# Two halves of the tensor engine for products of 64 rows or columns, and single-pass compressed scores, in a two-block transformer kernel

## The chip, the cores and the metric

The kernel runs on one core of a Trainium2 chip. The metric is the device time of one execution in microseconds (us). The core has a matrix engine (TensorE, PE in the profile, with PEld for the loads of its stationary operand), VectorE (DVE), ScalarE (ACT) and DMA queues that SyncE (SP) issues; GpSimd (POOL) is idle here. Products land in PSUM, in eight banks of 128 partitions by 512 float32 columns.

## The reference, cut to what matters

256 tokens of width 1024 pass through two blocks. The first block mixes tokens with gated linear attention, a convolution and differential attention, then applies routed experts. The second block has two layers, each an FFN, a token mixer and another FFN, with modulated norms. The edited code is in the token mixers:

```python
# first block, differential attention (4 heads, 2 maps of 64 channels), causal
a = softmax(q1 k1^T) - lam * softmax(q2 k2^T);  o = a v
# first block, gated linear attention (4 heads, keys 32, values 64)
o = scores v                       # scores with decays, causal
# second block, each layer: 8 query heads of 64, 2 key groups
kcmp = gelu(windows(kc) w1) w2     # 15 compressed keys per group
o  = g0 * softmax(q kcmp^T) vcmp   # compressed
o += g1 * softmax(q ks^T) vs       # selected blocks: all causal blocks at 256 tokens
o += g2 * softmax(q kw^T) vw       # window: the whole past at 256 tokens
# forgetting attention ("fox") and block attention ("moba"): 4 heads of 64 each
o = softmax(q k^T + bias) v
```

## The kernel before, in words

All weights are loaded as float32 and split into a high and a low part of type fp32r (`split`, L313 on ACT, L317 on DVE); a projection is then three products of fp32r (L337 to L339, L353 to L355). The small attention products are plain float32. The modulations (`ada_step`, L1059) multiply 32 columns at a time, four quarters of the tensor engine's columns one after another in the program.

PSUM is handed out in rings: `d`, `e` and `a` have two banks each, `n` and `m` one each (`ps`, L265). A tile of a ring takes the place of the one before it, in program order, when that one has been read for the last time. SBUF tiles work the same way: tiles of one tag share its `bufs` places.

The instructions of an engine do not run in program order. When the kernel is built, a planner goes through the program with its own costs for every instruction, takes on each engine the earliest in the program among those that it holds to be ready, and writes the waits. So projections and modulation steps stand between the steps of a softmax chain.

In `gla` (L808) two heads make one output tile; head 2p+e writes the partitions 64e to 64e+63. Its three products per head (L882 to L884) come head by head.

In `diff1` (L890) a pair of heads has two maps, m, on the partition halves of `qT` and `kT`. Map by map, two banks of ring `e` take the scores (L938, 128 columns, and L940, 256 columns), then a mask product, the maxima (L976, L977) and the exponentials (L487).

In `compressed` (L1308) the compressed keys of the two groups `KB` are multiplied head by head with the transposed queries (L1383): `qT` holds the high part of a query on the first 64 partitions and its low part on the other 64, `KB` holds the keys twice, so that one product sums both. It is a float32 product of 16 columns, 16 of them per layer. L1386 adds the mask.

In `selected` (L1413) the outer loop goes over the two key groups g. For each, four heads' scores and exponentials come first, then the probabilities are scaled (L1458, L1459), transposed four heads at a time (L1465), copied out of PSUM alternately by ACT and DVE (`cp`, L384 and L386), and multiplied with the values (L1469), into the partition half that belongs to the group:

```python
nc.tensor.matmul(po[t][gr, :], vn[:, kt, v0:v0 + 64], pT, start=False,
                 stop=(b == 1 and kt == t), skip_group_check=True)
```

The output tiles `po` are the two banks of ring `e`; they are copied out at L1299 and L1300.

In `causal` (L1472), called for fox and for moba in each layer, the heads 2e+hb lie on partition half hb. Half by half, two banks of ring `a` take the scores (L1485, L1486), fox's also a bias (L1488, L1489). Then, chunk by chunk, each head's probabilities are transposed through ring `e` (`prob_t`, L980) and multiplied with the values (L1510, L1511).

## Time and profile before

| | |
|---|---|
| three runs | 1467.1, 1471.0, 1472.7 us, median 1471.0 |
| profiled execution, first to last instruction | 1472.6 us |
| its own time | not listed apart from the runs; within 0.1 us of the span is the run of 1472.7 |
| PE busy | 1427.9 us, 97% |
| PEld busy | 1153.8 us, 78% |
| DVE busy | 1138.0 us, 77% |
| ACT busy | 854.0 us, 58% |
| DMA read | 324.13 MB, 221 GB/s over the span |

Busy time is the union of an engine's recorded instructions. A product's record includes its way through the array, so that the records of consecutive products overlap; how fast they follow each other is read from their starts. A product of plain float32 is recorded twice, once for each pass.

### The profile page before, as it was taken

The numbers are of one execution on the slowest core, as the hardware profiler recorded it, in microseconds if no ns is written. First come the engines' busy times: TensorE is split into PE (matmuls) and PEld (weight loads), VectorE is DVE, ScalarE is ACT, GpSimd is POOL, SyncE is SP. The second block draws the span as 40 slices with busy tenths as digits, with TensorE's granted clock in tenths as the row PEclk, the third lists the DMA queues.
The fourth block names the chain that finished last, engine by engine and source line by source line (L and its number), as shares of the span: only waits on it lengthen the run. The fifth ranks groups of instructions, "written<-read, shape, count | busy, mean of one in ns | idle before, by whom it ended". The sixth has DMA issues, their size and how long they took to land.

```text
span 1472.6 us, 22249 instructions
## 1 busy us (share of the span) xinstructions
PE 1427.9 (97%) x8077; PEld 1153.8 (78%) x8077; DVE 1138.0 (77%) x2553; ACT 854.0 (58%) x1573; POOL 0.2 (0%) x4
## 2 busy tenths in 40 slices
PE   7999699999999999999999999999999999999997
PEld 6756478778888888656888888888887666888886
DVE  8997577988998657675899886997677575887664
ACT  7545376877655544544765556666545444766553
POOL 0000000000000000000000000000000000000000
PEclk9999899999999999999999999999999899999999
DMA  8735475987887547533388676886577542165452
GB/s 303 276 126 213 186 257 224 345 326 280 316 312 258 179 168 261 219 125 132 126 306 306 246 262 213 325 294 224 169 290 261 200 160 93 62 229 200 156 176 70
DMA packets 51396, 326.67 MB, mean 222 GB/s; under 512 B 6209, under 2 KB 7378, under 8 KB 18898
## 3 DMA queue, kind: packets, MB, share of 16 engines
q1 hardware_dynamic: 50994, 325.00, 60.5%
q8 instruction: 65, 1.06, 0.3%
q14 instruction: 49, 0.40, 0.1%
q10 hardware_dynamic: 288, 0.20, 0.1%
HBM read 324.13 MB, written 1.05 MB: 221 GB/s over the span
## 4 chain that ended last, share of the span: by engine, by line
PE 79%; DVE 3%; ACT 2%; DMA 1%; issue 0%; DVEq 0%; ACTq 0%; SPq 0%
PE psd L337 12%; PE psa L337 10%; PE pse L337 10%; PE psd L339 6%; PE psa L339 6%; PE pse L339 5%; PE psd L353 2%; PE psd L354 2%; PE psm L1059 2%; PE psd L355 2%; PE pse L1469 2%; PE psd L1718 1%; PE psd L1719 1%; PE psd L1717 1%; DVE lo L317 1%; ACT hi L313 1%
## 5 line engine op out<-in xcount | busy, mean ns | idle before, releaser
L317 DVE TENSOR_TENSOR lo<-raw,hi 128x512 fp32r<-128x512 f32 x992 | 603.4, 636 | 162.3 <-ACT hi L313 158.5
L313 ACT ACTIVATE hi<-raw 128x1024 fp32r<-128x1024 f32 (+3 forms) x498 | 484.3, 978 | 343.5 <-PE psd L337 79.3
L337 PE MATMUL psd<-hl,hi 128*128 128x512 f32 x624 | 228.1, 406 | 8.0 <-DVE hl L641 6.8
L339 PE MATMUL psd<-hl,lo 128*128 128x256 f32 x656 | 186.3, 287 | 0.0
L337 PE MATMUL psa<-hl,hi 128*128 128x512 f32 x464 | 164.8, 396 | 1.1 <-ACT hi L313 1.1
L337 PE MATMUL pse<-hl,hi 128*128 128x512 f32 x464 | 164.1, 395 | 1.0 <-DVE w L610 0.7
L337 PEld LDWEIGHTS psd<-hl,hi 128*128 128x128 f32 x624 | 119.4, 193 | 40.0 <-ACT hi L313 8.5
L339 PE MATMUL pse<-hl,lo 128*128 128x256 f32 x512 | 143.0, 280 | 0.0
L339 PE MATMUL psa<-hl,lo 128*128 128x256 f32 x496 | 138.4, 281 | 0.0
L339 PEld LDWEIGHTS psd<-hl,lo 128*128 128x128 f32 x656 | 126.9, 193 | 2.7 <-DVE aP L1459 0.8
L337 PEld LDWEIGHTS psa<-hl,hi 128*128 128x128 f32 x464 | 87.1, 188 | 21.5 <-ACT hi L313 1.7
L337 PEld LDWEIGHTS pse<-hl,hi 128*128 128x128 f32 x464 | 87.2, 188 | 21.5 <-issue 1.2
L339 PEld LDWEIGHTS pse<-hl,lo 128*128 128x128 f32 x512 | 96.7, 189 | 0.3
L339 PEld LDWEIGHTS psa<-hl,lo 128*128 128x128 f32 x496 | 93.6, 189 | 1.4 <-DVE lo L317 0.8
L1088 DVE SCALAR_TENSOR_TENSOR acc<-araw,cact,acc 128x512 f32<-128x512 f32 x118 | 85.5, 744 | 0.8 <-DMA araw<-wada 0.8
L353 PE MATMUL psd<-hi,hl 128*128 128x512 f32 (+3 forms) x224 | 85.2, 380 | 0.8 <-ACT hl L375 0.4
L354 PE MATMUL psd<-lo,hl 128*128 128x512 f32 (+3 forms) x224 | 83.9, 375 | 0.0
L355 PE MATMUL psd<-hi,hl 128*128 128x512 f32 (+3 forms) x224 | 83.2, 374 | 0.0
L337 PE MATMUL psd<-hT,hi 128*128 128x512 f32 x220 | 77.6, 395 | 0.0
L337 PE MATMUL psa<-hT,hi 128*128 128x512 f32 x220 | 77.4, 394 | 0.0
L339 PE MATMUL psd<-hT,lo 128*128 128x256 f32 x264 | 74.2, 281 | 0.0
L339 PE MATMUL psa<-hT,lo 128*128 128x256 f32 x264 | 74.1, 281 | 0.0
(562 smaller groups left out, 2628.2 us busy)
## 6 DMA issues: line engine op xcount, KB each, us to landing
raw<-w SPq DMA_DIRECT2D x88, 1024.0 KB, 4.9
araw<-wada SPq DMA_DIRECT2D x64, 1024.0 KB, 6.2
raw<-w SPq DMA_DIRECT2D x64, 704.0 KB, 4.1
raw<-egu SPq DMA_DIRECT2D x32, 1024.0 KB, 4.9
raw<-edn SPq DMA_DIRECT2D x16, 1024.0 KB, 4.9
raw<-w2n SPq DMA_DIRECT2D x12, 1024.0 KB, 6.4
raw<-cw SPq DMA_DIRECT2D x8, 1024.0 KB, 6.9
araw<-wadb SPq DMA_DIRECT2D x8, 1024.0 KB, 5.8
```

What stands on the lines that cost most here:

```text
L313: nc.scalar.activation(hi[:, f:g], src[:, f:g], AF.Copy)
L317: ins = nc.vector.tensor_tensor(lo[:, f:g], src[:, f:g], hi[:, f:g].bitcast(F32), OP.subtract)
L337: nc.tensor.matmul(ps[:M, :].rearrange("p (a b) -> p a b", a=2), hi[:, o:o + M], xhl[:, k0 + k, :, :], start=st, stop=False)
L339: nc.tensor.matmul(ps[:M, 0:256], lo[:, o:o + M], xhl[:, k0 + k, 0, :], start=False, stop=sp)
L353: nc.tensor.matmul(o, xh, wh, start=st, stop=False)
L354: nc.tensor.matmul(o, xh, wl, start=False, stop=False)
L355: nc.tensor.matmul(o, xl, wh, start=False, stop=sp)
L1059: self.nc.tensor.matmul(self.ada_acc[32 * j:32 * j + 32, :], lhsT, rhs[:, 512 * j:512 * j + 512], start=start, stop=stop, tile_position=(0 ...
L1088: nc.vector.scalar_tensor_tensor(acc[:, w], raw[:, w], self.cact[:, c, 0:1], acc[:, w], OP.mult, OP.add)
L1469: nc.tensor.matmul(po[t][gr, :], vn[:, kt, v0:v0 + 64], pT, start=False, stop=(b == 1 and kt == t), skip_group_check=True)
L1717: nc.tensor.matmul(pg, xh(c), wh, start=(c == 0), stop=False)
L1718: nc.tensor.matmul(pg, xh(c), wl, start=False, stop=False)
```

## The change

It reorders products on half the tensor engine so that the two halves alternate in the program, and computes the compressed scores from keys in two fp32r parts. Comments are also removed.

- `gla`: the two heads of an output tile alternate, each with its column half named.
- `diff1` and `causal`: the scores of both partition halves come together, before any mask; the second half's two banks come from another ring (`d` in `diff1`, `e` in `causal`). The products themselves are the same.
- `causal`: both heads of a chunk are transposed first, then their value products alternate.
- `selected`: the outer loop goes over head pairs rp, the inner one over the groups g, so that a transposed tile holds two heads of each group; the value product of 512 columns becomes two of 256, one per half. The probabilities are scaled in the order of use. The ring of `aP1` has six places instead of four.
- `compressed`: the keys become a high and a low part of 16 columns each; one fp32r product of 32 columns per head and token tile takes the place of the float32 product of 16, and one more addition per token tile joins the parts. Two buffers share the places of others.

```diff
@@ gla
-            for e in range(2):
-                h = 2 * p + e
...
-                nc.tensor.matmul(po[r, 0:P], gv[:, 0, c], SA[:, h, :], start=True, stop=True)
-                nc.tensor.matmul(po[r, P:256], gv[:, 0, c], SX[:, h, :], start=True, stop=False)
-                nc.tensor.matmul(po[r, P:256], gv[:, 1, c], SA[:, 4 + h, :], start=False, stop=True)
+            for t, S_, o, q, st, sp in ((0, SA, 0, 0, True, True), (0, SX, 0, P, True, False), (1, SA, 4, P, False, True)):
+                for e in range(2):
+                    h = 2 * p + e
+                    nc.tensor.matmul(po[64 * e:64 * e + 64, q:q + P], gv[:, t, 64 * h:64 * h + 64], S_[:, o + h, :], start=st,
+                                     stop=sp, tile_position=(0, 64 * e))
@@ diff1
+            pms = [[self.ps(ring), self.ps(ring)] for ring in "ed"]
+            for e in range(2):
+                h = 2 * hp + e
+                for i, (q, n) in enumerate(((0, P), (P, 256))):
+                    for m in range(2):
+                        r = slice(64 * m, 64 * m + 64)
+                        nc.tensor.matmul(pms[m][i][:, e * n:e * n + n], qT[r, h, q:q + P], kT[r, h, 0:n], start=(e == 0),
+                                         stop=False, skip_group_check=True)
             for m in range(2):
-                r = slice(64 * m, 64 * m + 64)
-                p0, p1 = self.ps("e"), self.ps("e")
...
+                p0, p1 = pms[m]
                 self.mask_pair(p0, p1)
@@ compressed
-        Zc = [T([P, 16, 32], "Zc", 2) for i in range(2)]
+        Zc = [T([P, 16, 32], "apT", 3) for i in range(2)]
...
-        KB = T([P, 32], "KB")
-        nc.vector.tensor_copy(KB, pkc[:, 0:32])
+        KB = T([P, 2, 2, 16], "KB", 1, F32R)
+        kv = pkc[:, 0:32].rearrange("p (g k) -> p g k", g=2)
+        nc.scalar.activation(KB[:, :, 0, :], kv, AF.Copy)
+        nc.vector.tensor_tensor(KB[:, :, 1, :], kv, KB[:, :, 0, :].bitcast(F32), OP.subtract)
...
-                o = t * P + h * 16
-                kc = KB[:, 16 * (h % 2):16 * (h % 2) + 16]
-                nc.tensor.matmul(pc[:, o:o + 16], qT[:, h, t * P:(t + 1) * P].bitcast(F32), kc, start=True, stop=True)
+                o = t * 256 + h * 32
+                nc.tensor.matmul(pc[:, o:o + 32], qT[:, h, t * P:(t + 1) * P], KB[:, h % 2].rearrange("p a k -> p (a k)"),
+                                 start=True, stop=True)
...
-            nc.vector.tensor_tensor(SC[:, t], pc[:, t * P:(t + 1) * P].rearrange("p (h k) -> p h k", h=8),
-                                    self.k["cmask"][:, None, 16 * t:16 * t + 16].to_broadcast([P, 8, 16]), OP.add)
+            pv = pc[:, t * 256:(t + 1) * 256].rearrange("p (h a k) -> p h a k", h=8, a=2)
+            nc.vector.tensor_tensor(SC[:, t], pv[:, :, 1], self.k["cmask"][:, None, 16 * t:16 * t + 16].to_broadcast([P, 8, 16]),
+                                    OP.add)
+            nc.vector.tensor_tensor(SC[:, t], SC[:, t], pv[:, :, 0], OP.add)
@@ selected
-        for g in range(2):
-            gr = slice(64 * g, 64 * g + 64)
-            su = T([P, 2, 4, 2], "su", 2)
+        for rp in range(2):
+            su = T([P, 2, 2, 2, 2], "su", 2)
             P0, P1 = [], []
-            for rp in range(2):
+            for g in range(2):
...
-                    w1 = T([P, 2, 256], "aP1", 4)
+                    w1 = T([P, 2, 256], "aP1", 6)
...
-            for r in range(4):
-                for b in range(2):
-                    nc.vector.tensor_scalar(P0[r][:, b], P0[r][:, b], su[:, 0, r, b:b + 1], None, OP.mult)
-                    nc.vector.tensor_scalar(P1[r][:, b], P1[r][:, b], su[:, 1, r, b:b + 1], None, OP.mult)
             for b in range(2):
+                for i in range(4):
+                    for t, w in ((0, P0[i]), (1, P1[i])):
+                        nc.vector.tensor_scalar(w[:, b], w[:, b], su[:, t, i // 2, i % 2, b:b + 1], None, OP.mult)
+
                 for t, kt in ((0, 0), (1, 0), (1, 1)):
...
-                    v0 = P * (1 + b) + 64 * g
-                    nc.tensor.matmul(po[t][gr, :], vn[:, kt, v0:v0 + 64], pT, start=False,
-                                     stop=(b == 1 and kt == t), skip_group_check=True)
+                    for g in range(2):
+                        v0 = P * (1 + b) + 64 * g
+                        nc.tensor.matmul(po[t][64 * g:64 * g + 64, 256 * rp:256 * rp + 256], vn[:, kt, v0:v0 + 64],
+                                         pT[:, 256 * g:256 * g + 256], start=False, stop=(b == 1 and kt == t and rp == 1),
+                                         tile_position=(0, 64 * g), skip_group_check=True)
@@ causal
+        pms = [[self.ps(ring), self.ps(ring)] for ring in "ae"]
+        for e in range(2):
+            for i, (q, n) in enumerate(((0, P), (P, 256))):
+                for hb in range(2):
+                    r = slice(64 * hb, 64 * hb + 64)
+                    nc.tensor.matmul(pms[hb][i][:, e * n:e * n + n], qT[r, e, q:q + P], kT[r, ko + e, 0:n], start=(e == 0),
+                                     stop=False, skip_group_check=True)
         for hb in range(2):
-            r = slice(64 * hb, 64 * hb + 64)
-            p0, p1 = self.ps("a"), self.ps("a")
...
+            p0, p1 = pms[hb]
...
+            pTs = []
             for hb in range(2):
...
-                pT = self.prob_t(w0, w1)
-                nc.tensor.matmul(po[r, 0:256], v[:, 0, vo + 64 * h:vo + 64 * h + 64], pT[:, 0:256], start=True, stop=False)
-                nc.tensor.matmul(po[r, P:256], v[:, 1, vo + 64 * h:vo + 64 * h + 64], pT[:, 256:384], start=False, stop=True)
+                pTs.append(self.prob_t(w0, w1))
+            for t in range(2):
+                for hb in range(2):
+                    o = vo + 64 * (2 * e + hb)
+                    nc.tensor.matmul(po[64 * hb:64 * hb + 64, t * P:256], v[:, t, o:o + 64], pTs[hb][:, 256 * t:256 + P * t],
+                                     start=(t == 0), stop=(t == 1), tile_position=(0, 64 * hb))
```

## Rows read from the trace of the kernel before

**Rows 1.** The page: busy time and share of each engine, and the chain.
```profile
PE 1427.9 (97%) x8077; PEld 1153.8 (78%) x8077; DVE 1138.0 (77%) x2553; ACT 854.0 (58%) x1573; POOL 0.2 (0%) x4
...
PE 79%; DVE 3%; ACT 2%; DMA 1%; issue 0%; DVEq 0%; ACTq 0%; SPq 0%
```

**Rows 2.** Stretches: length, busy us of PE, PEld, DVE, ACT, POOL; clock, DMA.
```profile
84.00:115.00 31.00, 29.39 (x169) 16.61 (x162) 26.93 (x68) 12.95 (x50) 0.00 (x0) 1.00 0.50 174
600.00:630.00 30.00, 27.85 (x205) 20.93 (x206) 19.19 (x62) 17.15 (x50) 0.00 (x0) 0.89 0.61 241
630.00:710.00 80.00, 79.89 (x388) 50.33 (x387) 49.50 (x116) 35.39 (x97) 0.00 (x0) 1.00 0.35 123
```

**Rows 3.** Longest waits of PE, whole span: us in total, times, longest.
```profile
PE psd L337 <- DVE hl L641: 6.8, 1, 6.8
```

**Rows 4.** Instructions by line: count, busy us, mean ns, idle before.
```profile
L1469 PE MATMUL pse<-apT,vn 128*64 128x512 f32 x48 | 23.8, 608 | 0.1
L386 DVE COPY apT<-psa 128x512 f32<-128x512 f32 x12 | 8.3, 690 | 12.0 <-PE psa L1465 11.8
L384 ACT ACTIVATE apT<-psa 128x512 f32<-128x512 f32 x12 | 7.2, 596 | 29.9 <-PE psa L1465 28.1 <-DVE lo L317 1.8
```

**Rows 5.** PE in order of time, selected branch, layer 0: start, us.
```profile
629.99 0.60 PE L1465 MATMUL psa<-blob,aP 128*128 128x128 f32 x4
...
631.06 1.93 PE L1469 MATMUL pse<-apT,vn 128*64 128x512 f32 x4
...
657.36 1.07 PE L1469 MATMUL pse<-apT,vn 128*64 128x512 f32 x2
```

**Rows 6.** PE in order of time, first block's first scores.
```profile
83.69 1.06 PE L1059 MATMUL psm<-araw,cact 128*32 128x512 f32 x8
84.69 0.48 PE L938 MATMUL pse<-dT,dT 64*128 64x128 f32 x2
...
86.19 0.28 PE L969 MATMUL pse<-k_maskb,k_identb 128*128 128x256 bf16 x1
```

**Rows 7.** PE in order of time, fox's values in layer 0.
```profile
687.26 0.65 PE L1510 MATMUL psn<-w,n 128*64 128x256 f32 x2
...
688.54 0.33 PE L984 MATMUL pse<-blob,aP 128*128 128x128 f32 x1
...
690.45 0.66 PE L1510 MATMUL psn<-w,n 128*64 128x256 f32 x4
...
691.26 0.37 PE L1485 MATMUL psa<-qT 64*128 64x128 f32 x1
```

**Rows 8.** All engines in order of time, start of fox in layer 0.
```profile
674.41 0.48 PE L1485 MATMUL psa<-kd 64*128 64x128 f32 x2
...
677.00 0.68 DVE L1300 TENSOR_TENSOR hl<-pse,hl 128x512 fp32r<-128x512 f32 x1
```

**Rows 9.** PE in order of time, gated attention's values.
```profile
109.22 0.43 PE L882 MATMUL psa<-gSA,gv 128*64 128x128 f32 x2
...
110.02 0.33 PE L984 MATMUL pse<-blob,dP 128*128 128x128 f32 x1
```

**Rows 10.** Stretches, line 1383 alone: length, busy of PE, PEld; clock, DMA.
```profile
580.00:720.00 140.00, 4.62 (x32) 4.70 (x32) 0.98 0.41 151
1140.00:1270.00 130.00, 4.82 (x32) 4.89 (x32) 0.96 0.37 132
```

**Rows 11.** Stretches of the lower clock, columns as in Rows 2.
```profile
616.90:623.70 6.80, 6.80 (x26) 5.79 (x26) 3.80 (x11) 2.58 (x7) 0.00 (x0) 0.50 0.01 5
1173.30:1180.00 6.70, 6.70 (x27) 5.83 (x26) 3.74 (x10) 2.52 (x7) 0.00 (x0) 0.50 0.01 2
```

**Rows 12.** One line's instructions: duration in ns, least, median, most.
```profile
L1386 DVE TENSOR_TENSOR SC<-psn,k_cmask x4: 280/286/292, 619.1 to 1176.1; 128x128 f32<-128x128 f32 x4
```

**Rows 13.** PE in order of time, one modulation step in the first block.
```profile
114.93 1.05 PE L1059 MATMUL psm<-araw,cact 128*32 128x512 f32 x2 [0.44 <-DMA araw<-wada]
...
117.19 1.06 PE L1059 MATMUL psm<-araw,cact 128*32 128x512 f32 x6
```

More of the change, by code (lines that the diff above doesn't have):

```diff
@@ L1460, in selected @@
             for b in range(2):
+                for i in range(4):
+                    for t, w in ((0, P0[i]), (1, P1[i])):
+                        nc.vector.tensor_scalar(w[:, b], w[:, b], su[:, t, i // 2, i % 2, b:b + 1], None, OP.mult)
                 for t, kt in ((0, 0), (1, 0), (1, 1)):
                     pt = self.ps("a")
[L1463 to L1465 removed]
+                    for i in range(4):
+                        src = P0[i][:, b] if t == 0 else P1[i][:, b, kt * P:(kt + 1) * P]
+                        nc.tensor.transpose(pt[:, i * P:(i + 1) * P], src, ident)
@@ L1478, in causal @@
         w0s = T([P, 2, 2, P], "aP0", 3)
-        for hb in range(2):
-            r = slice(64 * hb, 64 * hb + 64)
-            p0, p1 = self.ps("a"), self.ps("a")
-            for e in range(2):
-                h = 2 * e + hb
-                s0, s1 = p0[:, e * P:e * P + P], p1[:, e * 256:e * 256 + 256]
-                nc.tensor.matmul(s0, qT[r, e, 0:P], kT[r, ko + e, 0:P], start=(e == 0), stop=False, skip_group_check=True)
-                nc.tensor.matmul(s1, qT[r, e, P:256], kT[r, ko + e, :], start=(e == 0), stop=False, skip_group_check=True)
-                if NB is not None:
-                    nc.tensor.matmul(s0, sel[0:96, h, :], NB[0:96, 0:P], start=False, stop=False, skip_group_check=True)
-                    nc.tensor.matmul(s1, sel[0:96, h, :], NB[0:96, :], start=False, stop=False, skip_group_check=True)
+        pms = [[self.ps(ring), self.ps(ring)] for ring in "ae"]
[5 more added lines that the diff above has]
+                                     stop=False, skip_group_check=True)
+        for hb in range(2):
+            p0, p1 = pms[hb]
+            if NB is not None:
+                for e in range(2):
+                    for p, n in ((p0, P), (p1, 256)):
+                        nc.tensor.matmul(p[:, e * n:e * n + n], sel[0:96, 2 * e + hb, :], NB[0:96, 0:n], start=False, stop=False,
+                                         skip_group_check=True)
             self.mask_pair(p0, p1)
             n0, n1 = self.neg_max(p0, p1)
-            w1s = T([P, 2, 256], "aP1", 4)
+            w1s = T([P, 2, 256], "aP1", 6)
             for e in range(2):
```

22 lines of the change are left out of this document (5 added, 17 removed).

## The prediction

> **What bounds the kernel now.** I read the page first, then a table of the stages that hold the edited code, then the instructions of each edited line. The page shows TensorE (PE) busy for 1427.9 of 1472.6 us, and the chain that ended last lies on PE for 79% of the span, far ahead of VectorE (DVE), ScalarE (ACT) and DMA [rows 1]. What counts is the same reading stage by stage. In the second block's attention (630 to 710 us, layer 0) PE has next to no gap, while DVE and ACT are at about 60% and 45% [rows 2]: where the softmax chain makes PE wait, the planner has put projections there. In the stretch of the compressed attention (600 to 630) PE stood still for 2.2 of 30 us. In the first block (84 to 115) DVE is busy 26.9 of 31 us, nearly as full as PE. The longest wait of PE for anything is 6.8 us and lies in routing and FFN code, outside the change [rows 3]. So a microsecond taken off PE's queue is a microsecond off the span as long as the projections still fill the gaps; it is worth less in the first block.
>
> Every fp32 product is recorded as two passes: the 24 products of line 1469 stand as 48 records [rows 4].
>
> **The change part by part.** The sum is made against the profiled span, 1472.6 us, 1.6 above the median 1471.0 of the three runs.
>
> *Values of the selected and window branch (L1469).* Today a group is one or two products of 512 columns into one half of the columns: four passes are recorded with 1.93 us, two with 1.07 [rows 5], so 0.43 per pass and 0.21 of start and end. There are nine groups of four and six of two, 9 x 1.93 + 6 x 1.07 = 23.8 us, the line's whole busy time [rows 4]. After, each product is split in two of 256 columns on the two halves, from the same transposed tile, so both halves are ready together and the planner has no reason to part them. That halves of the columns do run at once the trace shows twice: the modulations' eight 512-column passes on four quarters take 84.69 - 83.69 = 1.00 us [rows 6], and four 256-column and four 128-column passes that happen to alternate halves take 691.26 - 690.45 = 0.81 us, where others take 688.54 - 687.26 = 1.28 [rows 7]. Halved passes give 1.07 and 0.64 per group, 13.5 in all: **10.3 us saved**. Ends: 0 if the halves queue, 11.9 if start and end halve too.
>
> *Values of fox and moba (L1510, L1511).* Eight groups; four already take the paired 0.81, the other four 1.04 to 1.29, the first of [rows 7] among them. All at 0.81 would save 1.5. The two halves come from different transposes, which are copied out one after the other, so the planner may part them again: I take **0.7**, ends 0 and 1.5.
>
> *Scores on 64 rows (L938/940, L1485/1486).* Twelve groups of eight passes, at best 86.19 - 84.69 = 1.50 us each [rows 6], six pairs of 3.0. No row shows two row halves at work at once. Lower end for a pair: both streams overlap fully, 1.5. Upper end: no overlap, 3.0. Between them lies the case in which the weight loads go one by one: single-pass products of 128 columns follow each other at (0.60 - 0.27)/3 = 0.11 us (line 1465, [rows 5], one alone taken as 0.27), so 16 loads need 1.8. I take 1.7, saving 1.3, nearest to that and to what column halves do. But a pair must also stay together. The two heads' banks now come from two rings. For fox the second ring is held by the sparse branch's output: today its scores start at 674.41 and the last copy out of those banks ends at 677.00 + 0.68 [rows 8]. In the first block's second head pair the d banks are free early, the e banks late. I count these three pairs as torn (no saving), and the first block's first pair and moba's two, which all wait for the same transposes, as kept: **3.9**, ends 0 and 9.0. The Trainium skill, "TensorE: Matmul & The Clock Gate" (Part 3, measured speedup), has four row tiles at 3.07 times one; an estimate from that page, 0.77 of ideal, would make a pair 1.95 and this term 3.2 instead of 3.9. No row here shows row tiles.
>
> *Values of the gated attention (L882 to L884).* Six passes take 110.02 - 109.22 = 0.80 us [rows 9]; there are four such groups, two of which already ran side by side, 2.4 in all. Two paired groups make 1.6: **0.8**, ends 0 and 0.8.
>
> *Compressed scores (L1383).* 32 passes of 16 columns take 4.62 and 4.82 us [rows 10]. After, 16 single passes remain, each again with 128x128 weights, and at 0.11 us per load (above) take 1.8 + 0.27 = 2.0: **5.4** saved; 1.9 if they run at half clock as in [rows 11].
>
> *Clock.* The granted clock falls to 0.50 (1.2 GHz) in the second half of these 16-column products, for 6.8 us in each layer [rows 11]; the rest of the attention stages has it at 1.00, as the stretch 630 to 710 us [rows 2]. Each takes 3.4 us of full-speed work, of which the term above has 1.0 (32 loads at 0.11 would be 3.6). With the stretch of thin products less than half as long the clock may stay up: at most 2 x 2.4 = 4.8, at least 0; I take half, **2.4**.
>
> *Added work.* Keys are now split by an ACT copy and a DVE subtraction, and the scores need two more DVE additions per layer, 0.29 us each [rows 12]; with 0.3 for the split this lengthens the chain scores - softmax - values by some 0.9 us per layer. Projections cover part; if that cover is gone it costs 1.8. I charge **0.9**. Larger rings for the probabilities, shared buffers and the new order of normalizations add no instruction; I put them at 0, hidden by DVE's free 40%.
>
> *Sum.* 10.3 + 0.7 + 3.9 + 0.8 + 5.4 + 2.4 = 23.5 off PE. Half of the first block's 1.3 + 0.8 is lost to DVE, 1.0. In the second block the transposes now stand closer behind each other and wait for copies; I take a tenth of the rest, 2.1. Net 23.5 - 0.9 - 1.0 - 2.1 = 19.5: 1453 against the profile, **1452 us** as timed.
>
> **The rivals.**
> - *All of it lands*: pairs stay, the clock stays up, nothing waits: 10.3 + 1.5 + 9.0 + 0.8 + 5.4 + 4.8 = 31.8, so 1439. For: PE without gaps. Against: the two rings.
> - *The planner tears the pairs*: it orders each engine by its own costs, not by the program. For: the modulations' quarters are written together too, yet one product (two passes) ran alone for 1.05 us and the other three (six passes) 1.2 us after it [rows 13]. Then only L1469 and L1383 gain, the clock still falls: 15.7 less 0.9 less 1.4 is 13.4, so 1458. This is also the case in which the change does not do what it says.
> - *The gain turns into waits*: PE reaches the transposes earlier and stands until they are copied out, 0.69 us on DVE and 0.60 on ACT [rows 4]. Two copies at a time serve a group every 0.33 us, while transposes (0.44) and a paired product (0.5) need 0.94; so the copies' rate does not bind, but their latency in a ring of two banks may. Then little beyond the compressed scores remains: 1466. The Trainium skill, "TensorEngine Tiling (Array Packing)" (PSUM Bottleneck), warns that tiling speeds up the products and not the copies out of PSUM, and that these may then bind. By that rule the time would be this rival's 1466; the rates of [rows 4] speak against it.
> - *Slower*: PE with shorter work and more waiting is granted 0.50 of its clock more often. Place: the value groups and softmax gaps, 630 to 710 and the same in layer 1. Price: 3.4 us per stretch like those of [rows 11]. With the torn-pair gain, six further falls reach 1478.4, 0.5% slower. Against: the other stages hold 1.00 through waits of the same kind.
>
> **How the numbers follow.** Forecast 0.52, all lands 0.15, torn 0.15, turned into waits 0.12, slower 0.06. Half a percent, 7.4 us, is about what a measurement of this kernel can tell from no change: 1463.6 to 1478.4 is the same. Faster is 0.52 + 0.15 + 0.15 = 0.82, same 0.12, slower 0.06. The forecast's own range is 1447 to 1458 (scores 0 to 6, clock 0 to 4.8). The range for 8 in 10 runs from "all lands" to "turned into waits", with a microsecond on either side: 1438 to 1467.
>
> **What would show it.** Right: L1469's successor in groups of about 1.07 and 0.64 us, the halves starting together; the compressed scores in about 2 us; row-half scores starting in twos; granted clock 1.00 past the compressed scores; PE's gaps in the attention stages grown by less than 3 us per layer. Wrong: column halves that follow each other (then 10.3 is gone), a row pair at 3.0, scores of one half standing alone with projections between, new waits of PE on ACT or DVE copies of more than 5 us per layer, or several stretches at 0.50.

## The result, and the profile after

The changed kernel takes 1452.3 us (median of four runs, 1451.8 to 1456.9) where the kernel before takes 1470.0 beside it: a ratio of 0.9881, 95% interval 0.9862 to 0.9899. That is 17.7 us less. The forecast was 1452, from 19.5 us off a kernel of 1471.0; the total agrees to the microsecond, the gain to 2 us. The terms behind it do not all agree, and the parts turned out not to add. Most of this text is about that.

The page and the stretches of the profiled execution after (its own time 1456.9 us, the longest of the four runs), to be read against [rows 1] and [rows 2]:

```profile
PE 1411.1 (97%) x8093; PEld 1145.8 (79%) x8093; DVE 1138.2 (78%) x2557; ACT 856.0 (59%) x1575; POOL 0.2 (0%) x4
...
PE 79%; DVE 2%; ACT 2%; DMA 1%; issue 0%; DVEq 0%; ACTq 0%; SPq 0%
```

```profile
84.00:115.00 31.00, 28.09 (x135) 14.78 (x131) 24.99 (x65) 12.09 (x48) 0.00 (x0) 0.94 0.40 149
600.00:630.00 30.00, 26.98 (x200) 16.94 (x191) 20.35 (x66) 18.46 (x56) 0.00 (x0) 0.94 0.72 280
630.00:710.00 80.00, 79.80 (x451) 56.19 (x451) 55.58 (x136) 40.38 (x110) 0.00 (x0) 1.00 0.33 118
```

The span lost 17.5 us and PE's busy time 16.8. What left PE's queue left the span; the chain lies on PE for 79% as before, and 630 to 710 us still has 79.8 busy of 80. The gain is not spread evenly. Measured from the first product of one norm's sum of squares (L463, L473) to that of the next, the two token mixers of the second block are 28.7 us shorter (170.5 to 158.5 and 169.9 to 153.2), the FFNs behind them 6.0 longer (190.7 to 195.8 and 188.1 to 189.1), and the first block with its experts 5.0 longer (357.4 to 362.4; three other kernels with the same score edit there are 1.6 to 2.5 longer). The list of PE's waits (total, times, longest) shows nothing new in the attention; its longest outside routing is still that of [rows 3], with another releaser:

```profile
PE psd L337 <- ACT hi L313: 7.0, 2, 6.6
```

The edited lines after, by line and shape; the first three answer to [rows 4] (L1469, L386, L384), the fourth to L1383 of [rows 10]:

```profile
L1475 PE MATMUL pse<-apT,vn 128*64 128x256 f32 x96 | 13.8, 396 | 0.1
...
L386 DVE COPY apT<-psa 128x512 f32<-128x512 f32 x12 | 8.3, 690 | 4.2 <-PE psa L1470 4.1
...
L384 ACT ACTIVATE apT<-psa 128x512 f32<-128x512 f32 x12 | 7.2, 599 | 18.5 <-PE psa L1470 17.7 <-ACT hi L313 0.8
...
L1386 PE MATMUL psn<-KB,qT 128*128 128x32 f32 x32 | 3.7, 257 | 0.0
```

**Selected values.** 23.8 us became 13.8. In order of time (start, us; answers to [rows 5]) twelve, eight and four half-width passes take 1.52, 1.08 and 0.65 us. The forecast had 1.07 for eight and 0.64 for four.

```profile
632.85 1.52 PE L1475 MATMUL pse<-apT,vn 128*64 128x256 f32 x12
...
636.14 1.08 PE L1475 MATMUL pse<-apT,vn 128*64 128x256 f32 x8
...
638.90 0.65 PE L1475 MATMUL pse<-apT,vn 128*64 128x256 f32 x4
```

**Scores on 64 rows, the first block** (answers to [rows 6]). The first head pair stays together: its two banks (`psd`, `pse`) alternate, and 16 passes take 84.89 - 83.12 = 1.77 us, where two groups one after the other take 3.0. That is the first row of this case that shows both row halves at work at once; 1.7 had been assumed. The second pair is torn: only `psd` passes stand in its first runs, with other work behind each, and eight passes cost 0.64 + 1.06 us; `pse` follows from 96.58 on.

```profile
83.12 0.49 PE L939 MATMUL psd<-dT,dT 64*128 64x128 f32 x2
83.39 0.37 PE L939 MATMUL pse<-dT,dT 64*128 64x128 f32 x1
83.45 0.38 PE L939 MATMUL psd<-dT,dT 64*128 64x256 f32 x1
...
84.59 0.38 PE L939 MATMUL pse<-dT,dT 64*128 64x256 f32 x1
84.89 0.28 PE L970 MATMUL pse<-k_maskb,k_identb 128*128 128x256 bf16 x1
...
89.66 0.71 PE L939 MATMUL psd<-dT,dT 64*128 64x128 f32 x4
90.30 0.28 PE L970 MATMUL psd<-k_maskb,k_identb 128*128 128x256 bf16 x1
90.51 1.13 PE L939 MATMUL psd<-dT,dT 64*128 64x256 f32 x4
```

**Fox and moba in layer 0** (answer to [rows 7] and [rows 8]). Fox's first half (`psa`) runs alone for 1.5 us, the second (`pse`) 3 us later in two pieces, with the first half's bias and mask products and a modulation before it and bias products between its pieces. Moba's first half is scattered over 680 to 685 us and meets the second only partly. The values still come in pieces of two and six or, once, eight.

```profile
670.90 1.57 PE L1492 MATMUL psa<-kd 64*128 64x128 f32 x8
672.41 0.50 PE L1499 MATMUL psa<-NB,k_selb 96*128 96x128 bf16 x4
...
673.06 1.04 PE L1060 MATMUL psm<-araw,cact 128*32 128x512 f32 x2
674.04 0.71 PE L1492 MATMUL pse<-kd 64*128 64x128 f32 x4
674.68 0.28 PE L1499 MATMUL pse<-NB,k_selb 96*128 96x128 bf16 x2
674.89 1.13 PE L1492 MATMUL pse<-kd 64*128 64x256 f32 x4
...
680.61 0.92 PE L1492 MATMUL psa<-qT 64*128 64x128 f32 x4
...
682.83 0.65 PE L1524 MATMUL psn<-w,n 128*64 128x256 f32 x2
...
683.89 0.86 PE L1524 MATMUL psn<-w,n 128*64 128x256 f32 x6
...
685.16 0.37 PE L1492 MATMUL pse<-qT 64*128 64x128 f32 x1
...
686.50 0.87 PE L1524 MATMUL psn<-w,n 128*64 128x256 f32 x8
```

What holds moba's second half back shows when all engines are read in order of time. Its banks are those of ring `e`, through which fox's probabilities are transposed. The copy of the last of them ends at 685.27 + 0.56 = 685.83, and the half's 256-column scores start at 685.88, by the profile released by that copy:

```profile
685.27 0.56 DVE L386 COPY w<-pse 128x384 f32<-128x384 f32 x1 [1.50 <-PE pse L987]
...
685.88 0.29 PEld L1492 LDWEIGHTS pse<-qT 64*128 64x128 f32 x2 [0.20 <-DVE w L386]
```

**Gated attention and compressed scores** (answer to [rows 9] and [rows 10]). The gated values now run as one row of 24 passes from 116.10 to 117.56, 1.46 us (2.4 before). The 16 single passes of compressed scores take 622.71 - 621.01 = 1.70.

```profile
116.10 0.44 PE L882 MATMUL psa<-gSA,gv 128*64 128x128 f32 x4
...
117.56 0.62 PE L1060 MATMUL psm<-araw,cact 128*32 128x512 f32 x1
```

```profile
621.01 1.85 PE L1386 MATMUL psn<-KB,qT 128*128 128x32 f32 x16
622.71 0.48 PE L1447 MATMUL psa<-kT,qT 128*128 128x512 f32 x1
```

**The modulations**, which the change does not touch, grew. Before and after, the larger of their two groups (the other is 8.5 us in both):

```profile
L1059 PE MATMUL psm<-araw,cact 128*32 128x512 f32 x280 | 56.3, 612 | 4.6 <-DMA araw<-wada 4.3 <-DVE mod L1103 0.3
```

```profile
L1060 PE MATMUL psm<-araw,cact 128*32 128x512 f32 x280 | 60.0, 620 | 5.5 <-DMA araw<-wada 5.2 <-DVE mod L1104 0.3
```

They are the same 280 passes. Their four quarters run side by side where they stand next to each other, and one by one where something else stands between them, as in [rows 13]; the planner's new order has more of the latter (13 products of two passes stand alone before, 15 after, and one more is broken into its two passes). 20 of the passes also moved out of the two mixers into the FFNs behind them.

**The sum by what PE's order of time shows** (before minus after, us): selected values 10.0, compressed scores 5.7, first block's scores 1.4, fox and moba 0.8, gated values 0.9, values of fox and moba 0.1, together 18.9; modulations -3.7; that leaves 15.2, and 16.8 was found on PE. The remaining 1.6 were not traced to a line; products that the change does not touch differ by more than that either way (by the starts on PE, the projections take 6.0 us less and the selected branch's transposes 1.7 more).

### The profile page after: what moved, and what is told of

Read it like the earlier page. It is cut to its first block, busy times and chain, and to the rows that moved or that the text cites. A ratio compares the mean times of both kernels' runs of the same rounds, so it can differ in the third digit from the quotient of the medians.

```text
span 1455.1 us, 22278 instructions
## 1 busy us (share of the span) xinstructions
PE 1411.1 (97%) x8093; PEld 1145.8 (79%) x8093; DVE 1138.2 (78%) x2557; ACT 856.0 (59%) x1575; POOL 0.2 (0%) x4
## 3 DMA queue, kind: packets, MB, share of 16 engines
q8 instruction: 65, 1.06, 0.3%
## 4 chain that ended last, share of the span: by engine, by line
PE 79%; DVE 2%; ACT 2%; DMA 1%; issue 0%; DVEq 0%; ACTq 0%; SPq 0%
PE psd L337 12%; PE psa L337 11%; PE pse L337 10%; PE psd L339 7%; PE psa L339 6%; PE pse L339 5%; PE psd L353 2%; PE psm L1060 2%; PE psd L354 2%; PE psd L355 2%; PE psd L1732 1%; PE psd L1733 1%; PE psd L1731 1%; PE pse L1475 1%; PE pse L1754 1%; DVE lo L317 1%
## 5 line engine op out<-in xcount | busy, mean ns | idle before, releaser
L337 PE MATMUL psd<-hl,hi 128*128 128x512 f32 x624 | 225.0, 402 | 7.8 <-ACT hi L313 7.0
```

Of the source, the lines that this page charges most:

```text
L337: nc.tensor.matmul(ps[:M, :].rearrange("p (a b) -> p a b", a=2), hi[:, o:o + M], xhl[:, k0 + k, :, :], start=st, stop=False)
```

## Experiments: each part alone

Four kernels, each the kernel before with one part of the change. The diff of each is that part's hunk of the diff above (`sel_only` has the shared buffers of the compressed hunk too); where it decides, a line or two of it stands here.

**Compressed scores alone** (`cmp_only`).

```diff
-                nc.tensor.matmul(pc[:, o:o + 16], qT[:, h, t * P:(t + 1) * P].bitcast(F32), kc, start=True, stop=True)
+                nc.tensor.matmul(pc[:, o:o + 32], qT[:, h, t * P:(t + 1) * P], KB[:, h % 2].rearrange("p a k -> p (a k)"),
+                                 start=True, stop=True)
```

> The kernel before with the edit of the compressed attention alone. Theory (PE's queue counts, and the clock falls because of the thin products): the scores take 1.7 us instead of 4.6 to 4.8 per layer, 6 us in all, and neither layer falls to 0.50 of the clock in them, which returns up to 5 us more: 9 to 11 us, about 1460. Rival 1 (the falls do not depend on these products and only move elsewhere): 5 to 6 us, about 1464. Rival 2 (the added ACT and DVE steps lengthen the chain by as much): within 2 us of before.

Measured: 1466.5 us, ratio 0.9976 (0.9962 to 0.9989), 3.6 less. None of the three numbers was met. The theory had taken a fall of the clock in each layer from one profile; in this kernel's profile neither layer has one there, but over the runs the time at the lower clock is only some 4 us less (table below). PE's idle time in the mixers, 4.5 and 2.4 us against 4.2 and 2.4, does not show the longer chain of rival 2.

**Selected values alone** (`sel_only`).

```diff
-        for g in range(2):
+        for rp in range(2):
...
+                    for g in range(2):
...
+                                         pT[:, 256 * g:256 * g + 256], start=False, stop=(b == 1 and kt == t and rp == 1),
+                                         tile_position=(0, 64 * g), skip_group_check=True)
```

> The kernel before with the edit of the selected branch alone (value products in pairs of column halves, larger probability ring). Theory (PE's queue counts): the value products take 12.7 us instead of 22.7, and PE's gaps do not grow: 10 us, about 1460. Rival (PE reaches the transposes earlier and waits for the copies out of PSUM): less than 5 us, 1465 or more, with new waits of PE on lines 384 and 386.

Measured: 1461.1 us, ratio 0.9937 (0.9920 to 0.9954), 9.0 less. The line takes 14.4 us, so the halves of the columns run at once here too, and PE's idle time in the mixers does not grow (3.6 and 2.4 us): the theory, not the rival.

**Scores on 64 rows alone** (`scores_only`: both halves' scores first in `diff1` and `causal`, from two rings).

```diff
-                p0, p1 = self.ps("e"), self.ps("e")
+            pms = [[self.ps(ring), self.ps(ring)] for ring in "ed"]
...
-            p0, p1 = self.ps("a"), self.ps("a")
+        pms = [[self.ps(ring), self.ps(ring)] for ring in "ae"]
```

> The kernel before with the row-half scores alone (first block, fox and moba). Theory (most pairs are torn by the planner, since the two halves' banks come free at different times): the lines' time on PE falls by 2 to 3 us of 20.6, and the total by no more than that, 1467 to 1470. Rival 1 (the second ring lets the second half start before the first half's exponentials are done, so that the chain shortens): 5 us or more, 1465 or less. Rival 2 (the other ring's banks are held longer and others wait): slower than before by 2 us or more.

Measured: 1476.0 us, ratio 1.0034 (1.0020 to 1.0048): 5.9 more. The pairs are torn as in the changed kernel, so little is gained, and the modulations' larger group takes 60.2 us, 3.9 more than before. The number is rival 2's; its reason is not seen in the mixers, where PE is idle for 4.3 and 2.4 us as before (4.2 and 2.4).

**Values of the gated attention, fox and moba alone** (`vals_only`).

```diff
+            for t, S_, o, q, st, sp in ((0, SA, 0, 0, True, True), (0, SX, 0, P, True, False), (1, SA, 4, P, False, True)):
+                for e in range(2):
```

> The kernel before with alternating value products alone (gated attention, fox and moba). Theory: the gated attention's products take 1.5 us instead of 2.4; fox's and moba's stay at about 8 us, since the two heads' transposes are copied out at different times: 1 us in all, 1469, not to be told from before. Rival (pairs form, 6.5 us): 2.5 us.

Measured: 1470.4 us, ratio 1.0000 (0.9986 to 1.0013), as the theory had it in time. The gated values still stand in three groups and take 2.2 us, not 1.5. The row of 24 comes with the first block's score edit: `scores_only`, with the gated products in the old order, has it too, in 1.70 us.

By the ratios the four parts add to -7.8 us, each within about 2, so some 4 for the sum (the four intervals in quadrature); the whole change gave -17.5, within 2.7. Something between the parts is worth about 10 us, give or take 5. So the next kernels take one part out of the changed kernel.

## Experiments: one part taken out of the changed kernel

**Without the score edits** (`no_rows`), and **without the first block's score edit** (`no_diff`): the hunks of `diff1` and `causal` that move the scores taken back, or that of `diff1` alone.

```diff
-        pms = [[self.ps(ring), self.ps(ring)] for ring in "ae"]
...
+            p0, p1 = self.ps("a"), self.ps("a")
```

> The changed kernel with both score edits taken back (the first block's and the causal attention's scores one half after the other again); selected values, gated and causal values, compressed scores stay as changed. The three remaining parts, each alone against the kernel before, gave -9.0, 0 and -3.6 us, the score edits +5.9. Theory A (the score edits cost what they cost alone, because they push 14 modulation passes of layer 0 out of the mixer into the FFN behind it): 1452.3 - 5.9 = 1446.4 us, and the FFN behind layer 0 back to 190.6 us from 195.8. Rival B (the parts help each other, the score edits pay in company): the three parts add from the kernel before, 1470 - 12.6 = 1457.4 us. The middle, 1452, would say that the score edits are worth nothing in company.

> The changed kernel with the first block's scores alone as before; the causal attention's stay paired. Theory A: the first block is 2.5 to 3 us longer since the change, so taking its edit back gives 1452.3 - 2.8 = 1449.5 us, and the FFN behind layer 0 keeps its 195.8 us. Rival B (what is won in the first block, 1.4 us of the tensor engine, counts in company): 1453.7 us.

Measured: 1451.0 us without both (ratio 0.9867, 0.9843 to 0.9892), 1449.6 without the first block's (0.9861, 0.9835 to 0.9888). Neither theory's number for `no_rows` was met: it came out in the middle, which had been said to mean that the score edits are worth nothing in company. `no_diff` agrees with its theory A (1449.5): by the medians the first block's edit costs 2.7 us though it saves 1.4 on its own products. All three intervals overlap, so what the times show is that the score edits bring nothing; that they cost is not shown by them. The profiles tell more of the first block: with its experts it takes 359.0 to 362.4 us in the four kernels that have its score edit and no ordering edges (the change, `scores_only`, `no_cmp`, `no_sel`), and 356.3 to 358.3 in the six without that edit or any edges.

Where their saving goes the modulations' line shows, by stretches: the mixer of layer 0, the FFN behind it, the mixer of layer 1. First the changed kernel, then the one without score edits (columns after the length: PE, PEld, clock, DMA):

```profile
550.00:718.00 168.00, 15.20 (x62) 2.27 (x62) 0.99 0.45 168
716.00:912.00 196.00, 7.00 (x34) 1.20 (x34) 1.00 0.73 263
1098.00:1260.00 162.00, 15.21 (x70) 2.47 (x70) 1.00 0.48 174
```

```profile
547.00:712.00 165.00, 16.06 (x72) 2.70 (x72) 1.00 0.48 180
712.00:903.00 191.00, 3.86 (x20) 0.59 (x20) 1.00 0.72 259
1090.00:1257.00 167.00, 16.06 (x72) 2.69 (x72) 1.00 0.46 168
```

The reader is to see the second row of each. With the scores taken early, 14 more passes of modulations fall into the FFN, which is 195.8 us long instead of 191.4 (from norm to norm); the mixer before it is shorter by 1.9 only. In layer 1 the mixer is shorter by 4.0 and the FFN behind it, with 6 more passes, longer by 0.9. So in the second block the score edits win 5.9 us in the mixers and lose 5.3 behind them. The move happens with the score edits alone, too: the FFN of layer 0 takes 195.8 us there and 190.7 before.

**Without the compressed edit** (`no_cmp`): two passes of 16 columns again, in the changed kernel's buffers.

```diff
-                nc.tensor.matmul(pc[:, o:o + 32], qT[:, h, t * P:(t + 1) * P], KB[:, h % 2].rearrange("p a k -> p (a k)"),
-                                 start=True, stop=True)
+                nc.tensor.matmul(pc[:, o:o + 16], qT[:, h, t * P:(t + 1) * P].bitcast(F32), kc, start=True, stop=True)
```

> The changed kernel with the compressed scores again in two passes of 16 columns (with the changed kernel's buffers). Theory A (the edit is worth 2 x 1.8 us of tensor-engine time at the full clock, as it was alone: -3.6): 1452.3 + 3.6 = 1455.9 us, the step 3.5 us a layer at the full clock. Rival B (the thin products also bring the lower clock back, 3.4 to 6.8 us of it in one layer or both, at some 0.4 us of time each): 1458 to 1461 us, with a fall just behind the products in the trace. Rival C (the step lies beside the wait for the softmax anyway): 1452 us.

Measured: 1463.3 us, ratio 0.9952 (0.9935 to 0.9969): 11 more than the changed kernel, beyond even rival B's 1458 to 1461. Its trace has the step at both levels of the clock, in stretches that hold it (the line alone: PE, PEld, clock of the stretch):

```profile
605.00:640.00 35.00, 4.83 (x32) 4.91 (x32) 0.90 0.55 211
```

```profile
1160.00:1180.00 20.00, 3.64 (x32) 3.73 (x32) 1.00 0.60 236
```

In layer 0 the clock fell in the middle of the products, in layer 1 it did not. At 1.00 the 32 passes take 3.64 us and the 16 that replace them 1.85, so the edit itself is worth 1.8 a layer. The fall and its stretch (clock in the third column from the right):

```profile
619.20:625.90 6.70, 6.70 (x26) 5.79 (x26) 3.29 (x10) 2.15 (x7) 0.00 (x0) 0.50 0.01 5
```

**Without the selected edit** (`no_sel`): the outer loop over groups and the 512-column products again, and with them the four-place ring of `aP1` and a buffer of its own for `Zc`.

```diff
-        for rp in range(2):
+        for g in range(2):
...
-                    for g in range(2):
...
+                    nc.tensor.matmul(po[t][gr, :], vn[:, kt, v0:v0 + 64], pT, start=False,
+                                     stop=(b == 1 and kt == t), skip_group_check=True)
```

> The changed kernel with the selected blocks' products group by group again, as before the change; everything else as changed. The compressed edit was worth 3.6 us alone and 11 in company, and the three parts without the score edits gave 19.5 where they add to 12.6: two of them help each other. Theory A (the selected edit is worth its 10 us of tensor engine, alone 9.0, wherever it stands, and what did not add was the compressed edit's): 1452.3 + 9.0 to 10.0 = 1461.3 to 1462.3 us. Rival B (the selected and the compressed edit only pay in full together): the other three add from the kernel before, 1470 - 3.6 + 0.4 and 1.3 to 5.9 for the score edits, 1468 to 1473 us.

Measured: 1468.9 us, ratio 0.9992 (0.9979 to 1.0004). Rival B: in company the selected edit is worth 16.6 us, alone 9.0. Its line is as it was, 24.0 us, so 10 of the 16.6 are its own products. Most of the rest is other work that stands elsewhere. In the profiles the two mixers are 13 us longer than the change's (163.2 and 161.6 against 158.5 and 153.2): PE is idle 1.3 us more in the first, and the second holds 62 modulation passes in 15.4 us where the change has 58 in 12.5 and the others behind it. Of the 11 us of `no_cmp` 3.6 are the products' own, some 2 the clock's and 0.9 the modulations' (table below); some 4 stay open.

**What the parts share.** Two things in these runs are not any part's own. The first is the modulations' time (both groups of the line, by line and shape: 64.8 us before). The second is the time at the lower clock, for which the table has the mean over a kernel's runs (from each run's mean granted clock: twice the missing share of its span). Over 64 runs of the kernel before, the time is some 3.5 us longer with every 10 us of it.

| kernel | time against before, us (from the ratio) | modulations, us | time at the lower clock, us |
|---|---|---|---|
| before | 0 | 64.8 | 32 |
| compressed alone | -3.5 | 66.9 | 28 |
| selected alone | -9.3 | 66.7 | 34 |
| scores alone | +5.0 | 68.7 | 39 |
| values alone | 0 | 66.1 | 30 |
| all (the change) | -17.5 | 68.5 | 26 |
| all but scores | -19.6 | 65.1 | 23 |
| all but compressed | -7.1 | 69.4 | 32 |
| all but selected | -1.2 | 69.7 | 28 |

Every part alone disturbs the order that the planner had found for the modulations, at 1.3 to 3.9 us; the four costs add to 9.2, but the whole change pays 3.7 once. If a microsecond of modulations is one of time, that is 5.5 of the 10 us. At the lower clock the parts' differences from before add to about +4, the change has -6; at 0.35 us per us that is another 3 or 4. So up to 9 of the 10 have a place. Which order the planner falls into is not a property of any edit, and no run here changes the order alone with the products as before; that the modulations explain the missing sum is worked out from these rows, not shown by an edit of its own in this group. The next group has one (`no_rows_ada`): there 11.7 us of modulations bring 3.0 us of time, so the 5.5 is an upper bound.

## Experiments: pairs and quarters kept together

**Ordering edges on the pairs** (`glue_all`, `glue_scores`). The changed kernel, and each second-half product is given an edge to the first half's, of the kind that makes the planner place it behind and adds no wait. In `causal` the half whose banks come late is written first.

```diff
-                for hb in range(2):
+                prev = None
+                for hb in (1, 0):
...
-                    nc.tensor.matmul(pms[hb][i][:, e * n:e * n + n], qT[r, e, q:q + P], kT[r, ko + e, 0:n], start=(e == 0),
-                                     stop=False, skip_group_check=True)
+                    ins = nc.tensor.matmul(pms[hb][i][:, e * n:e * n + n], qT[r, e, q:q + P], kT[r, ko + e, 0:n], start=(e == 0),
+                                           stop=False, skip_group_check=True)
+                    if prev is not None:
+                        self.after(ins, prev)
+                    prev = ins
```

> The changed kernel with one thing added: ordering edges, without waits, that make the scheduler place the two halves of every score product and of every causal value product next to each other. Theory A (a pair only pays when its halves stand next to each other: 16 score passes in 1.77 us where they do, 3.0 to 3.4 where not): four causal score groups go from 13.2 to about 7.5 us, the first block's second from 3.4 to 1.8, the values from 7.9 to about 5: 10 us less on the tensor engine, some 7 of it in the time, 1445 us. Rival B (the first half now waits for the second half's banks and operands, and the modulations go elsewhere again): the passes shrink as said, but the engine stands still instead, 1452 us or more.

> The changed kernel with ordering edges on the score products alone; the causal value products stay as the scheduler places them. With edges on both, 1442.3 us, the scores took 7.9 us less of the tensor engine than in the changed kernel and the values 1.5 less. Theory A (each pair is worth what its passes save): 1442.3 + 1.5 = 1443.8 us. Rival B (the value edges carry the gain, by what they move elsewhere): 1449 us or more.

Measured: 1442.3 us with edges on scores and values (ratio 0.9812, 0.9788 to 0.9836), 1446.6 with edges on the scores alone (0.9841, 0.9828 to 0.9855). Against the changed kernel that is 10 and 5.7 us less. Fox's scores of `glue_all` in order of time, where 16 passes of both banks now take 665.98 - 664.18 = 1.80 us:

```profile
664.18 0.37 PE L1497 MATMUL pse<-kd 64*128 64x128 f32 x1
664.19 0.37 PE L1497 MATMUL psa<-kd 64*128 64x128 f32 x1
664.40 0.27 PE L1497 MATMUL pse<-kd 64*128 64x128 f32 x1
664.40 0.27 PE L1497 MATMUL psa<-kd 64*128 64x128 f32 x1
...
665.63 0.38 PE L1497 MATMUL pse<-kd 64*128 64x256 f32 x1
665.67 0.38 PE L1497 MATMUL psa<-kd 64*128 64x256 f32 x1
665.98 0.51 PE L1507 MATMUL psa<-NB,k_selb 96*128 96x128 bf16 x4
```

The two banks' passes start within 0.04 us of each other, twice 8 passes in the time of 8. The causal scores take 7.2 us instead of 13.2, the first block's 3.2 instead of 5.2, the values 6.4 instead of 7.9; the FFN behind layer 0 is back at 190.2 us. The rival's price, PE waiting for the late banks, did not come: the waits of PE in that layer are those of the changed kernel. PE's busy time:

```profile
PE 1393.9 (97%) x8093; PEld 1138.4 (79%) x8093; DVE 1137.2 (79%) x2557; ACT 854.1 (59%) x1575; POOL 0.2 (0%) x4
```

Theory A is right on the whole (1445 expected, 1442.3 found), but the gain does not stand where the pairs do. In the profiles the mixers are 2.4 us shorter than the changed kernel's, because the 20 modulation passes are back in them; the FFNs behind are 6.5 us shorter, and the first block is at 354.5 us, below all kernels without edges. So the edges show what this order is worth, pairs and displaced work together, and not the pairs alone. On how it splits between scores and values the runs are not clear: 1446.6 lies between theory A's 1443.8 and rival B's 1449, and the two kernels' intervals touch.

**Ordering edges on the modulations** (`no_rows_ada`: `no_rows`, and the three further quarters of a step are planned right behind the first; `glue_all_ada`: `glue_all` with the same).

```diff
-        for j in range(nj):
-            self.nc.tensor.matmul(self.ada_acc[32 * j:32 * j + 32, :], lhsT, rhs[:, 512 * j:512 * j + 512],
-                                  start=start, stop=stop, tile_position=(0, 32 * j))
+        def mm(j):
+            return self.nc.tensor.matmul(self.ada_acc[32 * j:32 * j + 32, :], lhsT, rhs[:, 512 * j:512 * j + 512],
+                                         start=start, stop=stop, tile_position=(0, 32 * j))
+        first = mm(0)
+        with self.tc.high_priority():
+            for j in range(1, nj):
+                self.after(mm(j), first)
```

> As no_rows, and the four quarters of each modulation step are kept next to each other in the order of the tensor engine (in no_rows 24 quarters stand alone and 46 in twos and threes; here 18 in twos and the rest in fours). Theory A (a quarter alone takes its whole 0.23 us, four together about 0.5): the modulations' 61 us fall by 10 us or so, and the time 5 to 10 us below that of no_rows, 1437 to 1441 us. Rival B (they wait for data of late loads in a block where the quarters apart filled gaps): the same as no_rows within 2 us.

> The changed kernel with ordering edges on the score and value pairs and with the modulations' quarters kept together. The two alone: the edges 1442.3 us (10 below the changed kernel), the quarters 1448.0 against 1451.0 without them (61.6 us of modulations became 49.8 on the tensor engine, idle time rose by 3). Theory A (they add): 1442.3 - 3 = 1439 us. Rival B (both take their gain from the same gaps): 1442 us or more.

Measured: 1448.0 us for the first (ratio 0.9845, 0.9821 to 0.9869; 1451.0 without the edges), 1440.0 for the second (0.9798, 0.9781 to 0.9814; 1442.3 without). The line in `no_rows` and in `no_rows_ada`:

```profile
L1058 PE MATMUL psm<-araw,cact 128*32 128x512 f32 x280 | 55.5, 615 | 5.0 <-DMA araw<-wada 4.7 <-DVE mod L1102 0.3
```

```profile
L1058 PE MATMUL psm<-araw,cact 128*32 128x512 f32 x280 | 43.8, 615 | 1.9 <-DMA araw<-wada 1.2 <-DVE mod L1107 0.7
```

This edit changes no product, only the order, and the same 280 passes cost 11.7 us less on PE: their price is set by their neighbours, as the sum above assumed. That this price is paid in time one for one, as the sum also assumed, is not borne out. Only 3.0 and 2.3 us arrive, which neither pair of intervals tells apart from nothing. Part of the rest stood as idle time of PE between products (3 us more in the first, 9 in the second, by the products' starts and ends); the time at the lower clock is also 7 to 10 us longer in both. `glue_all_ada` is the fastest kernel of this study by its median, 30 us below the kernel before, and not distinguishable from `glue_all`.

## Why the prediction was right, and where it was not

- **The bound.** Right. PE is without gaps in the second block's attention after as before, no new wait appeared there, and 16.8 us off PE were 17.5 off the span. In the first block, where a microsecond was to be worth less, it seems to have been worth less than nothing (below).
- **Selected values, 10.3.** Right: 10.0 by the line, with groups of 8 and 4 passes at the prices that were named (1.08 and 0.65), and some of 12.
- **Compressed scores, 5.4, and clock, 2.4.** The step got shorter by 5.7 in the profiles. The prediction knew that 1.0 us of each layer's old duration was the fall's (32 passes were to take 3.6 at the full clock, and 3.64 was measured), and counted it as saved all the same, 2.0 in the term and 2.4 beside it, 4.4 for the clock in all. The edit itself saves 1.8 a layer, 3.6. The old duration had been read from two layers that both had the fall. Across the profiles of this study a fall begins among or right behind the two-pass products in 5 of 10 layers (none in `sel_only`, which also has them), behind the single-pass ones in none of 18. So the clock term was of the right kind and about twice too large: over the runs the time at the lower clock went from 32 to 26 us, some 2 us of time at 0.35.
- **Scores on 64 rows, 3.9.** The price of a pair was right (1.77 and 1.80 for 1.7). The estimate that had been worked out from the Trainium skill ("TensorE: Matmul & The Clock Gate", Part 3), 1.95, was too high. The count was wrong: three pairs of six were to stay together, one did. The step that failed is "moba's two, which all wait for the same transposes, as kept": moba's first half starts at 680.61, its second at 685.16. Both wait for the same transposes, but the second half's banks are those of ring `e`, and they come free only when fox's transposed probabilities have been copied out (685.83 for the last). The prediction asked when the banks come free for fox and did not ask it for moba. 2.2 us were saved on these products, and in company they are worth nothing in time.
- **What was not in the sum.** The cost of moving other work. It put other work at nothing, with a tenth taken off for waits; in the second block there were no new waits, but the modulations became 3.7 us dearer, and 20 of their passes moved into the FFNs, 14 of them into one in which PE had been idle for 0.7 us and which became 5.1 longer. [rows 13] had been read as evidence on torn pairs alone; they were also the price list of this.
- **First block, 1.0 lost.** Too small, as far as the runs tell: without its score edit the kernel is 2.7 us faster, within overlapping intervals. Three things differ in the profiles with that edit and no edges. Up to the end of the experts the same 128 modulation passes take 24.1 to 24.2 us, and 21.5 to 22.5 without it (by the starts on PE); that alone does not decide, since in `glue_all` they take 24.3 and the block is shorter than any of these. PE is idle there for 21.8 to 22.9 us, and 19.8 to 21.3 without it. And the granted clock falls to 0.50 for 3.4 us at 107 us, in all four of these profiles and in none of the six without the edit (0.94 for the stretch 84 to 115, where [rows 2] had 1.00). Which of them costs how much is open.
- **Fox and moba's values, 0.7; gated values, 0.8.** 0.1 and 0.9; alone, both together gave 0, and the 0.9 needs the first block's score edit.
- **Added work, 0.9.** No row shows it as PE idle.
- **The rivals.** The torn pairs happened, for five of six score pairs and for the values; they did not give 1458: without any score edit the kernel takes 1451.0, so the difference lies in what the selected values and the compressed scores are worth in company, part of which is traced above and part open. The copies out of PSUM did not come to bind, as the rates had it; DVE's and ACT's copies after the transposes take 690 and 599 ns (690 and 596 before) and PE waits no longer for them (3.4 us in all, 4.7 before). The rule cited from the Trainium skill ("TensorEngine Tiling (Array Packing)", PSUM Bottleneck), which speaks of a fourfold speedup, did not decide here. The rival with more falls of the clock did not come true: none came where it was expected, 630 to 710 us, and the time at the lower clock got shorter. Two falls of 3.4 us are new in the profile after: the one in the first block, and one in layer 0 at 605 us, ahead of the compressed scores.

The gains that were too large (scores, clock, the values' 0.7) and the costs that were missing or too small (modulations, first block) pull the same way. The deductions for added work and waits (0.9 and 2.1), for which no row shows PE standing still in the second block, made up for part of them. The forecast was right in its main term, selected values, and lucky in the rest.

## What to carry to other kernels

Products on two halves of the array gained only where they stood next to each other in the engine's queue; where a planner orders that queue, alternating them in the program is not enough, and ordering edges took the same change from 1452 to 1442 us. To say whether a pair will stay together, ask for both halves when the operands are ready and when the output banks come free. When an edit moves work that a planner fits into gaps, count what else shares the queue, and measure each part both alone and taken out: 9.0 and 16.6 us for one edit say that neither number is the edit's own. A duration taken from a profile may hold the lower clock, so read the granted clock of its stretch before it goes into a sum.

## What the runs showed of the hardware

Two row halves of the array (64 rows each, 128 columns) ran fp32 passes at once: 16 passes of 128 and 256 columns took 1.77 to 1.80 us and 8 take 1.5, so the second half is nearly free. For column halves the rows show the same: eight half-width passes in 1.08 us, where four of full width on one half took 1.93.

The granted clock is not the same in every execution of a kernel. The falls to 0.50 that the two 16-column stretches of the kernel before had are present in some profiles and absent in others with the same products: in `no_cmp` layer 0 has one and layer 1 not, with 4.83 and 3.64 us for the same step. Behind the single-pass products none of 18 layers had it. Over 64 runs of the kernel before, 10 us more at the lower clock go with 3.5 us more time.
